# Where the first block tile of each channel mixer prepares the second one's weights

## The chip, the cores and the metric

The kernel runs on one core of a Trainium2 chip. Its time is the device time of one execution in microseconds (us); three executions of the kernel before gave 1180.54, 1180.71 and 1181.04 us, so their median is 1180.71 us. The engines named below are TensorE (PE in the profile, with its weight loads as PEld), VectorE (DVE), ScalarE (ACT), GpSimd (POOL) and SyncE (SP), which issues the loads of weights.

## The reference, cut to what matters

The program is a trunk of two layers over 512 tokens with a model width of 1024, in float32. Each layer has a mixer and then a channel mixer, a gated MLP with a short causal convolution on the gate. The change lies in the channel mixer:

```python
D_FF = ((8 * D_MODEL // 3 + 127) // 128) * 128      # 2816

def causal_dwconv(x, w, b):                         # width 3
    k = w.shape[0]; s = x.shape[1]
    xp = jnp.pad(x, ((0, 0), (k - 1, 0), (0, 0)))
    y = xp[:, 0:s] * w[0]
    for j in range(1, k):
        y = y + xp[:, j:j + s] * w[j]
    return y + b

def conv_ffn(h, w_up, conv_w, conv_b, w_down):
    u, g = jnp.split(h @ w_up, 2, axis=-1)
    g = causal_dwconv(g, conv_w, conv_b)
    return (jax.nn.silu(g) * u) @ w_down

x = x + conv_ffn(rmsnorm(x, norm_ffn_g[l]), ffn_w_up[l], ffn_conv_w[l], ffn_conv_b[l], ffn_w_down[l])
```

## The kernel before

Activations lie with features on the partitions and the 512 tokens along a row. Every float32 operand of a matmul is split into a high part (a cast to fp32r, on ScalarE, line 145) and a low part (the difference, on VectorE, line 146), and one product of two such pairs is three matmuls (lines 201 to 203). The 2816 columns of the hidden width are 22 tiles of 128. Tiles 0 and 1 are computed plainly. Tiles 2 to 21 are **block tiles**: the up and gate weights of a tile, cut into two halves of the 1024 input rows, are four blocks, the activations, cut into two halves of the tokens, are blocks too, and seven block products with sums of blocks (Winograd's form of Strassen's scheme) take the place of eight. In the code a11 and a12 are the halves of the up weights, a22 is a half of the gate weights, and s1 to s4 are the four sums that VectorE forms (line 1048 for each of the four). One block product is 12 matmuls of 256 columns.

`step` (line 966 on) is one block tile. Tile 2 is called the first step here, tile 3 the second, and so on. On TensorE a step is, in this order: a11's product into a PSUM tile r1; a12's into r2; s2's into r1; s1's into r3; s3's into r1; two down products; a22's product into r1; any further down products; s4's product, which adds to r3. The down products belong to `ffn_w_down`: each is a group of 512-column matmuls into a PSUM tile "tr", of which there are two. The first step has four such groups, of six matmuls each, the following steps two. r1 is used four times in a step, so each of its later uses needs ScalarE to have copied the result of the one before out of it (line 983 for the first, line 972 for the others). A "tr" tile is free again when ScalarE has copied it (`add`, line 834), after which GpSimd issues an accumulating DMA of the copy (line 838). r3 is read by VectorE after s1's product (line 1004) and again in the following step (line 1106), and s4's product may not add to it before the first of these reads.

While step j runs, ScalarE and VectorE also **prepare** the weights of tile j + 1 (`Forms`): `sums` forms s1 and s2, `split_second` splits s2, `sum_third` forms s3, `split_up` splits the 1024 columns of a11 and a12, `split_sums` splits s1 and s3 together, `sum_fourth` forms s4, `split_gate` splits a22, and `split_down` splits the tile's down weights. `split_fourth` (s4) stands at the head of the step that uses it. The preparation of the first block tile itself happens during the plain tiles. In the same time the **tail** of tile j − 1 runs (`Tail`): the rest of r3, the scaling by the norm's row, three taps of the convolution (line 770 on ScalarE, two at line 763 on VectorE), silu and the gating. The first step has no tail, since no block tile precedes it; in its place it splits the two hidden rows of the plain tiles.

The channel mixer is written inside a manual schedule: TensorE, ScalarE and VectorE execute their instructions in the order in which the code issues them, each engine in its own queue. So an instruction that waits holds back everything behind it on its engine. SyncE issues the loads as buffers come free.

Of the kernel before, what the change touches and what calls it, by code (L numbers as in the profile page):

```python
# [59 lines left out]
def trunk(  # L60
# [34 lines left out]
    def sb(tag, shape, dtype=F32):  # L95
        count[0] += 1
        return pool.tile(shape, dtype, tag=tag, name=f"{tag}{count[0]}", bufs=bufs[tag])

    def ps(tag):
        count[0] += 1  # L100
        return psum.tile([P, S], F32, tag=tag, name=f"p{tag}{count[0]}", bufs=pbufs[tag])
# [381 lines left out]
    with tc.manual_schedule(engines={mybir.EngineType.PE, mybir.EngineType.Activation, mybir.EngineType.DVE}):  # L483
# [20 lines left out]
        def step(products, os_, k, order):  # L504
            for a, b in order:
                for i, o in enumerate(os_):
                    c = slice(i * P, (i + 1) * P)
                    st, mv = kv[k][a], memT[k][b]
                    first, last = (k, (a, b)) == (0, order[0]), (k, (a, b)) == (KT - 1, order[-1])
                    if products == "keys":  # L510
                        nc.tensor.matmul(o, st[:, c], mv, start=first, stop=last)
                    else:
                        nc.tensor.matmul(o, mv[:, c], st[:, MEM:], start=first, stop=last)
# [12 lines left out]
        first, second = slice(0, MEM), slice(MEM, S)  # L526
# [13 lines left out]
        for q in range(KT // 2):  # L540
            k = 2 * q
            step("keys", ko, k, weights_last if q else ((0, 0), (1, 0), (0, 1)))
            if not q:
                step("values", vo, k, weights_last)
            if q < KT // 2 - 1:
                split(*parts_of[q + 1], memory_rows(q + 1, ("tr", "sc")[q % 2], range(2)))
                for j in (k + 2, k + 3):
                    split(*kv[j], kvraw[j])
            if q:
                step("values", vo, k, weights_last)  # L550
            step("keys", ko, k + 1, weights_last)
            if q == KT // 2 - 1:
                kws1 = [parts(kraw1[0], block=0)]
                keep(0, 0, ko)
                kws1.append(parts(kraw1[1], block=1))
            step("values", vo, k + 1, weights_last)
# [184 lines left out]
    class ChannelMixer:  # L741
# [222 lines left out]
        def step(self, j, w, nxt, tail, plain=None):  # L964
            def then(o, *names):
                for name in names if o is not None else ():
                    getattr(o, name)()

            def sum_products(o, r, w, i):

                self.products(r, w, self.t(i))
                A.copy(o, r[:, :H])  # L972

            new = Tail(self, j)
            late = self.load_late(LATE_ROW[j]) if j in LATE_ROW else None
            then(tail, "last_block", "scaled")
            if tail is not None:
                w.split_fourth()
            then(tail, "scaled_up")
            r1, r2, new.r3 = ps("mm"), ps("mm"), ps("sc")  # L980
            new.up, new.u3, new.pre = sb("t", [P, S]), sb("t", [P, S]), sb("t", [P, S])
            self.products(r1, w.a11, self.b(0, 0), True)
            A.copy(new.up[:, :H], r1[:, :H])
            if tail is None:
                self.keep(plain[0])
                w.split_down()
                V.tensor_tensor(out=plain[1], in0=plain[2], in1=plain[1], op=ALU.mult)
            then(tail, "first_tap", "second_tap", "third_tap")
            self.products(r2, w.a12, self.b(1, 0), True)
            V.tensor_tensor(out=new.up[:, :H], in0=new.up[:, :H], in1=r2[:, :H], op=ALU.add)  # L990
            sum_products(new.up[:, H:], r1, w.s2, 2)
            if tail is None:
                self.keep(plain[1])
                w.split_gate()
                w.split_fourth()
            then(tail, "silu")
            then(nxt, "sums")
            self.products(new.r3, w.s1, self.t(1), True)
            then(tail, "gated")
            then(nxt, "split_second", "sum_third")  # L1000
            sum_products(new.u3[:, :H], r1, w.s3, 3)
            then(tail, "split")
            then(nxt, "split_up")
            V.tensor_tensor(out=new.pre[:, H:], in0=new.u3[:, :H], in1=new.r3[:, :H], op=ALU.add)
            w.down_products(0, 2)
            then(nxt, "split_sums", "sum_fourth")
            w.add_down(0)
            then(nxt, "split_gate")
            w.add_down(1)
            then(nxt, "split_down")  # L1010
            sum_products(new.pre[:, :H], r1, w.a22, 4)
            w.down_products(2, 4)
            self.products(new.r3, w.s4, self.b(1, 1))
            w.add_down(2)
            w.add_down(3)
            if late is not None:
                self.late_row(LATE_ROW[j], late)
            return new, nxt
# [571 lines left out]
    sums = [[] for _ in range(TT)]  # L1590
# [109 lines left out]
```

## Time and profile before

| what | value |
|---|---|
| median of three runs | 1180.71 us |
| the profiled execution | 1180.69 us, its span 1178.7 us |
| TensorE busy | 1162.8 us (99%) |
| VectorE busy | 993.8 us (84%) |
| ScalarE busy | 748.1 us (63%) |
| GpSimd busy | 151.2 us (13%) |
| granted TensorE clock | 0.998 of full speed |
| first step of layer 0 | from 296.3 us of the span, its second step from 315.8 us |
| first step of layer 1 | from 851.3 us of the span |

Times in rows of a timeline are microseconds from the start of the span, followed by the duration of one instruction (or of several that follow each other, counted after an x), and in brackets by the idle time of the engine before it and what ended it. Line numbers are those of the kernel before; the change adds three lines inside `step`, so that line 972 keeps its number, 1004 becomes 1005 and lines from 1048 on become three higher.

### The profile page before, as it was taken

The page shows a single profiled execution, that of the slowest core. Times are in us where ns is not written, and L with a number is a line of the kernel's source. Part 1 is how long each engine was busy: PE and PEld are TensorE (multiplying, and loading weights), DVE is VectorE, ACT ScalarE, POOL GpSimd, SP SyncE. Part 2 cuts the span into 40 slices and gives each one's busy share as a digit, 9 for nine tenths or more (in the row PEclk, how much of TensorE's full clock was granted, in tenths as well). Part 3 has the DMA queues.
Part 4 walks back from the last instruction along what each step waited for, and adds up shares of the span by engine and source line. Part 5 has one row for each costly group of instructions (what it writes and reads, how often), then busy time and mean ns, then how long its engine had stood idle before and what let it go on. Part 6 is the DMA issues. An engine that isn't in the chain of part 4 may idle for free. (4 is left out here: it accounts for less than half of the span.)

```text
span 1178.7 us, 19339 instructions
## 1 busy us (share of the span) xinstructions
PE 1162.8 (99%) x7221; PEld 1036.8 (88%) x7221; DVE 993.8 (84%) x1776; ACT 748.1 (63%) x1347; POOL 151.2 (13%) x254
## 2 busy tenths in 40 slices
PE   9999999999999999999999999999999999999997
PEld 9988888888899999999888888778889999999986
DVE  6777788879899988888798888898989998888865
ACT  6548677657576655555576676776766765555545
POOL 1211101010121222111020000101010111111100
PEclk9999999999999999999999999999999999999999
DMA  8645315244458878776573313235345767777651
GB/s 283 224 110 147 80 55 152 67 152 125 129 155 179 213 174 197 194 172 144 148 218 108 90 55 104 95 95 178 110 133 147 159 148 177 177 179 171 134 162 72
DMA packets 204784, 171.27 MB, mean 145 GB/s; under 512 B 9256, under 2 KB 177934, under 8 KB 204690
## 3 DMA queue, kind: packets, MB, share of 16 engines
q1 hardware_dynamic: 184946, 123.93, 35.7%
q0 software_dynamic: 19168, 45.06, 18.9%
q8 instruction: 56, 0.92, 0.3%
q10 hardware_dynamic: 576, 1.05, 0.2%
q14 instruction: 38, 0.31, 0.1%
HBM read 133.09 MB, written 40.85 MB: 148 GB/s over the span
## 5 line engine op out<-in xcount | busy, mean ns | idle before, releaser
L201 PE MATMUL pmm<-u,wh 128*128 128x256 f32 (+1 forms) x992 | 334.8, 338 | 0.9 <-ACT t L972 0.7
L203 PE MATMUL pmm<-u,wl 128*128 128x256 f32 (+1 forms) x992 | 332.1, 335 | 0.0
L202 PE MATMUL pmm<-u,wh 128*128 128x256 f32 (+1 forms) x992 | 331.8, 334 | 0.0
L146 DVE TENSOR_TENSOR wl<-wr,wh 128x1024 fp32r<-128x1024 f32 (+4 forms) x166 | 186.2, 1122 | 69.6 <-ACT wh L145 69.2
L145 ACT CAST wh<-wr 128x1024 fp32r<-128x1024 f32 (+4 forms) x166 | 160.4, 969 | 71.6 <-PE pmm L202 30.1
L203 PEld LDWEIGHTS pmm<-u,wl 128*128 128x128 f32 x992 | 186.3, 188 | 18.9
L201 PEld LDWEIGHTS pmm<-u,wh 128*128 128x128 f32 x992 | 186.4, 188 | 17.8 <-ACT t L972 1.1
L202 PEld LDWEIGHTS pmm<-u,wh 128*128 128x128 f32 x992 | 186.5, 188 | 16.2 <-DVE u L146 0.5
L201 PE MATMUL ptr<-u,wh 128*128 128x512 f32 x272 | 106.9, 393 | 2.0 <-ACT bias L834 1.0
L202 PE MATMUL ptr<-u,wh 128*128 128x512 f32 x272 | 106.5, 392 | 0.5 <-DVE u L146 0.5
L203 PE MATMUL ptr<-u,wl 128*128 128x512 f32 x272 | 105.8, 389 | 0.0
L145 ACT CAST fh<-pt 128x512 fp32r<-128x512 f32 x120 | 74.8, 625 | 38.5 <-DVE pt L1048 37.2
L201 PE MATMUL pmm<-u,fh 128*128 128x256 f32 x320 | 89.0, 278 | 2.7 <-ACT t L972 2.7
L202 PE MATMUL pmm<-u,fh 128*128 128x256 f32 x320 | 88.6, 277 | 0.0
L972 ACT COPY t<-pmm 128x256 f32<-128x256 f32 x120 | 45.1, 376 | 68.5 <-PE pmm L203 68.4
L203 PE MATMUL pmm<-u,fl 128*128 128x256 f32 x320 | 88.4, 276 | 0.0
L146 DVE TENSOR_TENSOR fl<-pt,fh 128x512 fp32r<-128x512 f32 x120 | 82.4, 688 | 4.6 <-ACT fh L145 1.4
L763 DVE SCALAR_TENSOR_TENSOR t<-t,cols,t 128x511 f32<-128x511 f32 x88 | 65.9, 749 | 10.7 <-ACT t L770 9.2
L201 PEld LDWEIGHTS pmm<-u,fh 128*128 128x128 f32 x320 | 60.1, 188 | 5.6 <-ACT t L972 4.2
L201 PE MATMUL psc<-u,wh 128*128 128x256 f32 (+1 forms) x208 | 63.2, 304 | 0.0
L203 PE MATMUL psc<-u,wl 128*128 128x256 f32 (+1 forms) x208 | 63.0, 303 | 0.0
L202 PE MATMUL psc<-u,wh 128*128 128x256 f32 (+1 forms) x208 | 62.9, 303 | 0.0
(360 smaller groups left out, 2641.3 us busy)
## 6 DMA issues: line engine op xcount, KB each, us to landing
wr<-in_ffn_w_up_dram SPq DMA_DIRECT2D x46, 512.0 KB, 8.2
pt<-in_ffn_w_up_dram SPq DMA_DIRECT2D x40, 512.0 KB, 7.9
wr<-in_ffn_w_down_dram SPq DMA_DIRECT2D x32, 512.0 KB, 5.1
wr<-in_a_w_in_dram SPq DMA_DIRECT2D x20, 512.0 KB, 3.7
xspill<-bias POOLq DMA_DIRECT2D x32, 256.0 KB, 6.9
without_row<-bias POOLq DMA_DIRECT2D x24, 256.0 KB, 4.0
wr<-in_w_kv_dram SPq DMA_DIRECT2D x12, 512.0 KB, 3.8
without_row<-t POOLq DMA_DIRECT2D x24, 256.0 KB, 4.2
```

The costliest lines, as they stand in the source:

```text
L145: high = A.copy(hi, src) if on_act else V.tensor_copy(hi, src)
L146: low = V.tensor_tensor(out=lo, in0=src, in1=f(hi), op=ALU.subtract)
L201: nc.tensor.matmul(o, lh, rh, start=first, stop=False, skip_group_check=more)
L202: nc.tensor.matmul(o, lh, rl, start=False, stop=False, skip_group_check=more)
L203: nc.tensor.matmul(o, ll, rh, start=False, stop=last, skip_group_check=more)
L763: V.scalar_tensor_tensor(acc[:, n:], src[:, : S - n], self.fw[:, c * FT + j : c * FT + j + 1], acc[:, n:], op0=ALU.mult, op1=ALU.add,)
L972: A.copy(o, r[:, :H])
```

## The change

In the first step of each of the two channel mixers, and nowhere else, the preparation of the next tile's weights is issued later. Before, its eight parts were spread over the step: the sums ahead of s1's product, then `split_second` and `sum_third` ahead of s3's product and its copy, and so on. Now seven of them are issued together, behind the copy of s3's product (line 972) and behind the copies of the first two down products (line 834), and the eighth, `split_down`, is issued at the end of the step. `split_up` also comes ahead of `split_second` now. The following steps are as they were. Nothing is added or removed: each engine has the same instructions.

```diff
-            then(nxt, "sums")
+            first, rest = (None, nxt) if tail is None else (nxt, None)
+            then(first, "sums")
             self.products(new.r3, w.s1, self.t(1), True)
             then(tail, "gated")
-            then(nxt, "split_second", "sum_third")
+            then(first, "split_second", "sum_third")
             sum_products(new.u3[:, :H], r1, w.s3, 3)
             then(tail, "split")
-            then(nxt, "split_up")
+            then(first, "split_up")
             V.tensor_tensor(out=new.pre[:, H:], in0=new.u3[:, :H], in1=new.r3[:, :H], op=ALU.add)
             w.down_products(0, 2)
-            then(nxt, "split_sums", "sum_fourth")
+            then(first, "split_sums", "sum_fourth")
             w.add_down(0)
-            then(nxt, "split_gate")
+            then(first, "split_gate")
             w.add_down(1)
-            then(nxt, "split_down")
+            then(rest, "sums", "split_up", "split_second", "sum_third", "split_sums", "sum_fourth", "split_gate")
+            then(first, "split_down")
             sum_products(new.pre[:, :H], r1, w.a22, 4)
             w.down_products(2, 4)
             self.products(new.r3, w.s4, self.b(1, 1))
             w.add_down(2)
             w.add_down(3)
+            then(rest, "split_down")
```

ScalarE's queue in the first step of layer 0, before. The numbers behind a name are buffers: pmm_3215 is r1, the ptr tiles hold the down products, pt_2791 holds the gate weights as loaded and pt_2792 the sums, wr_3015 the up weights of the next tile and wr_3017 its down weights; fh and wh are the high parts.

```order
L145 CAST fh_3277<-pt_2792 128x512
L145 CAST fh_3295<-pt_2792 128x512
L972 COPY t_3219<-pmm_3215 128x256
L145 CAST wh_3313<-wr_3015 128x1024
L145 CAST wh_3332<-pt_2792 128x1024
L834 COPY bias_3337<-ptr_3318 128x512
L145 CAST fh_3340<-pt_2791 128x512
L834 COPY bias_3344<-ptr_3325 128x512
L145 CAST wh_3347<-wr_3017 128x512
L972 COPY t_3220<-pmm_3215 128x256
L834 COPY bias_3390<-ptr_3364 128x512
L834 COPY bias_3393<-ptr_3371 128x512
```

And the same place of ScalarE's queue with the change:

```order
L145 CAST fh_3277<-pt_2792 128x512
L972 COPY t_3219<-pmm_3215 128x256
L834 COPY bias_3321<-ptr_3307 128x512
L834 COPY bias_3324<-ptr_3314 128x512
L145 CAST wh_3329<-wr_3015 128x1024
L145 CAST fh_3333<-pt_2792 128x512
L145 CAST wh_3338<-pt_2792 128x1024
L145 CAST fh_3343<-pt_2791 128x512
L972 COPY t_3220<-pmm_3215 128x256
L834 COPY bias_3386<-ptr_3360 128x512
L834 COPY bias_3389<-ptr_3367 128x512
L145 CAST wh_3392<-wr_3017 128x512
```

The copy of s3's product (t_3219) moved ahead of `split_second` (fh_3295, now fh_3333), and the first two copies of down products ahead of `split_up` and `split_sums`; the cast of the next tile's down weights moved from ahead of the copy of a22's product (t_3220) to the end.

VectorE's queue in the same step, before; lines 1048 are the four sums, line 1004 the first read of r3 (psc_3217), fl and wl the low parts.

```order
L146 TENSOR_TENSOR fl_3278<-pt_2792,fh_3277 128x512
L1048 TENSOR_TENSOR pt_2792<-pt_2791 128x512
L1048 TENSOR_TENSOR pt_2792<-pt_2792,wr_3015 128x512
L146 TENSOR_TENSOR fl_3296<-pt_2792,fh_3295 128x512
L1048 TENSOR_TENSOR pt_2792<-wr_3015,pt_2791 128x512
L146 TENSOR_TENSOR wl_3314<-wr_3015,wh_3313 128x1024
L1004 TENSOR_TENSOR t_3220<-t_3219,psc_3217 128x256
L146 TENSOR_TENSOR wl_3333<-pt_2792,wh_3332 128x1024
L1048 TENSOR_TENSOR pt_2792<-wr_3015,pt_2792 128x512
L146 TENSOR_TENSOR fl_3341<-pt_2791,fh_3340 128x512
L146 TENSOR_TENSOR wl_3348<-wr_3017,wh_3347 128x512
```

And with the change:

```order
L146 TENSOR_TENSOR fl_3278<-pt_2792,fh_3277 128x512
L1005 TENSOR_TENSOR t_3220<-t_3219,psc_3217 128x256
L1051 TENSOR_TENSOR pt_2792<-pt_2791 128x512
L1051 TENSOR_TENSOR pt_2792<-pt_2792,wr_3015 128x512
L146 TENSOR_TENSOR wl_3330<-wr_3015,wh_3329 128x1024
L146 TENSOR_TENSOR fl_3334<-pt_2792,fh_3333 128x512
L1051 TENSOR_TENSOR pt_2792<-wr_3015,pt_2791 128x512
L146 TENSOR_TENSOR wl_3339<-pt_2792,wh_3338 128x1024
L1051 TENSOR_TENSOR pt_2792<-wr_3015,pt_2792 128x512
L146 TENSOR_TENSOR fl_3344<-pt_2791,fh_3343 128x512
L146 TENSOR_TENSOR wl_3393<-wr_3017,wh_3392 128x512
```

The read of r3 moved ahead of all sums, and the low part of the up weights (wl) ahead of the low part of s2 and of the third sum; TensorE, GpSimd and SyncE keep their order.

## The prediction

> **What bounds the kernel now.** I read the page first, then what TensorE waits for, then a table by stretches, then the timelines of the three engines around the first step.
>
> ```profile
> span 1178.7 us, 19339 instructions
> PE 1162.8 (99%) x7221; PEld 1036.8 (88%) x7221; DVE 993.8 (84%) x1776; ACT 748.1 (63%) x1347; POOL 151.2 (13%) x254
> PE pmm L201 <- ACT t L972: 3.4, 4, 1.3
> PE ptr L201 <- ACT bias L834: 1.0, 1, 1.0
> PE ptr L201 <- ACT t L834: 1.0, 1, 1.0
> ```
>
> TensorE is the bound; time is won only where it stands still. The three rows of waits (us in total, times, longest) are the largest it has on other engines in the whole span, and both kinds end on a ScalarE copy that the change moves.
>
> ```profile
> 296.30:314.30 18.00, 15.06 (x97) 12.79 (x96) 15.06 (x22) 10.23 (x17) 1.08 (x2) 1.00 0.26 82
> 326.60:338.90 12.30, 12.30 (x99) 11.81 (x97) 11.69 (x19) 8.44 (x17) 2.24 (x5) 1.00 0.63 177
> ```
>
> Columns: stretch, length, busy time of PE, PEld, DVE, ACT, POOL, granted clock, DMA. The first row holds most of layer 0's first step: TensorE idles 2.94 of 18.00 us. The second is a later step: TensorE never idles, but VectorE is busy for 11.69 of 12.30 us. VectorE is the engine that runs late next.
>
> ```profile
> 306.50 0.69 DVE L1048 TENSOR_TENSOR pt<-pt 128x512 f32<-128x512 f32 x1
> 307.22 0.69 DVE L1048 TENSOR_TENSOR pt<-pt,wr 128x512 f32<-128x512 f32 x1
> 304.56 1.14 ACT L145 CAST fh<-pt 128x512 fp32r<-128x512 f32 x2
> 307.94 0.62 ACT L145 CAST fh<-pt 128x512 fp32r<-128x512 f32 x1 [2.25 <-DVE pt L1048]
> 308.47 0.37 ACT L972 COPY t<-pmm 128x256 f32<-128x256 f32 x1
> 308.73 1.05 ACT L145 CAST wh<-wr 128x1024 fp32r<-128x1024 f32 x1
> 309.98 1.05 ACT L145 CAST wh<-pt 128x1024 fp32r<-128x1024 f32 x1 [0.20 <-DVE pt L1048]
> 310.93 0.58 ACT L834 COPY bias<-ptr 128x512 f32<-128x512 f32 x1
> 311.41 0.62 ACT L145 CAST fh<-pt 128x512 fp32r<-128x512 f32 x1
> 307.16 0.39 PE L203 MATMUL ptr<-u,wl 128*128 128x512 f32 x1
> 308.89 0.38 PE L201 MATMUL pmm<-u,fh 128*128 128x256 f32 x1 [1.34 <-ACT t L972]
> 311.56 0.50 PE L201 MATMUL ptr<-u,wh 128*128 128x512 f32 x1 [1.02 <-ACT bias L834]
> ```
>
> ScalarE waits 2.25 us for VectorE's second sum, and behind that cast stands the copy of r1 (308.47) for which TensorE waits 1.34 us with a22's product. Two long casts later comes the copy of a down product (310.93), for which TensorE waits 1.02 us with the third group. Layer 1 has the same waits (the counts above).
>
> **What the change removes.** The copy of r1 now follows the two casts of 304.56 and ends near 306.0, before TensorE is there. The first two copies of down products follow at once. So TensorE goes on from its last row of the second group (307.16) without either wait. How much earlier would the second step begin if nothing else were late? Its rows are these; the rows of the other engines are for the next part:
>
> ```profile
> 315.82 0.28 PE L201 MATMUL pmm<-u,wh 128*128 128x256 f32 x1
> 326.74 0.28 PE L201 MATMUL psc<-u,fh 128*128 128x256 f32 x1
> 328.10 0.28 PE L201 MATMUL pmm<-u,wh 128*128 128x256 f32 x1
> 311.29 1.22 DVE L146 TENSOR_TENSOR wl<-pt,wh 128x1024 fp32r<-128x1024 f32 x1
> 312.42 0.68 DVE L1048 TENSOR_TENSOR pt<-wr,pt 128x512 f32<-128x512 f32 x1
> 316.02 0.42 DVE L1106 TENSOR_TENSOR t<-t,psc 128x256 f32<-128x256 f32 x1 [0.20 <-PE psc L203]
> 316.36 0.68 DVE L1109 TENSOR_TENSOR t<-t,rb 128x512 f32<-128x512 f32 x1
> 316.96 0.68 DVE L146 TENSOR_TENSOR fl<-pt,fh 128x512 fp32r<-128x512 f32 x1
> 317.65 0.82 ACT L770 ACTIVATE t<-t,cols 128x512 f32<-128x512 f32 x1
> 318.50 1.54 DVE L763 SCALAR_TENSOR_TENSOR t<-t,cols,t 128x511 f32<-128x511 f32 x2 [0.85 <-ACT t L770]
> 319.96 0.41 DVE L990 TENSOR_TENSOR t<-t,pmm 128x256 f32<-128x256 f32 x1
> 320.29 0.68 DVE L1048 TENSOR_TENSOR pt<-pt 128x512 f32<-128x512 f32 x1
> 321.01 0.69 DVE L1048 TENSOR_TENSOR pt<-pt,wr 128x512 f32<-128x512 f32 x1
> 322.38 0.69 DVE L146 TENSOR_TENSOR fl<-pt,fh 128x512 fp32r<-128x512 f32 x1
> 324.70 1.23 DVE L146 TENSOR_TENSOR wl<-wr,wh 128x1024 fp32r<-128x1024 f32 x1 [0.26 <-ACT wh L145]
> 325.84 0.41 DVE L1004 TENSOR_TENSOR t<-t,psc 128x256 f32<-128x256 f32 x1
> ```
>
> The second step runs from 315.82 to 328.10: 12.28 us. Its s4 product, 12 matmuls of 256 columns, takes 1.36 (326.74 to 328.10); seven such products are 9.52, which leaves 2.76 for its two down groups, 0.23 for each of 12 matmuls. From 307.16 the new first step then goes: 0.23 to a22's product at 307.39; 1.36; two more down groups, 2.76; s4's product, 1.36; and the second step begins at 312.87 instead of 315.82. That is 2.95 us, more than the 2.36 of the two idle times, since a wait also slows the matmul behind it (0.38 against 0.28 at 308.89).
>
> **What is late next.** VectorE has the same work to do in less time, and its preparation now starts later, behind ScalarE's copies. I time the new order with the old durations. An instruction lets the next start after 0.60 (512 columns: 316.36 to 316.96), 1.13 to 1.14 (1024: 311.29 to 312.42, 324.70 to 325.84) or 0.33 (256: 319.96 to 320.29) on VectorE; a wait across engines adds 0.03 to 0.05 (316.36 + 0.68 = 317.04 would release the tap; 317.65 + 0.82 = 318.47, and VectorE starts at 318.50).
>
> - The second down group ends at 307.16 + 0.39 = 307.55. ScalarE copies it at 307.58 and casts the up weights 0.48 later (as 310.93 to 311.41): 308.07 to 309.11.
> - VectorE, which has read r3 and made two sums by 308.3, waits for that cast: low part of the up weights at 309.15, low part of s2 at 310.29, third sum 310.89 to 311.58.
> - ScalarE's cast of s1 and s3 waits for that third sum, 311.62 to 312.67, and VectorE's low part for the cast: 312.70. Then without a gap: fourth sum 313.84, gate 314.44, down weights 315.05, rest of r3 315.65, scaling 315.98 to 316.67.
> - Tap on ScalarE 316.71 to 317.53; two taps on VectorE from 317.56, 1.46 to the next (318.50 to 319.96): line 990 at 319.02, first sum 319.35, second (0.72 later, as at 320.29) 320.07 to 320.76; cast on ScalarE, low part of s2 at 321.46; third sum, low part of the hidden row and low part of the up weights at 322.06, 322.66 and 323.27; read of r3 at 324.41, done at 324.82.
>
> Before, that read (line 1004) was at 325.84, done at 326.25, and TensorE came to s4's product at 326.74: 0.44 to spare after the release. Now TensorE would be there at 312.87 + 10.92 = 323.79 and has to wait until 324.87, 1.08 us in all. (A part falls earlier in the step. On ScalarE, behind the cast of 311.62, stand the gate's cast, the copy of a22's product, two copies of down products and two casts: 0.95 + 0.53 + 0.26 + 2 × 0.48 + 2 × 0.53 by the starts above. So the first copy of r1 in the second step comes at 315.4, done at 315.75, while TensorE is due with s2's product at 312.87 + 2.72 = 315.59. Some 0.2 us are waited there and are then missing from the second wait.) s4's product starts 326.74 − 324.87 = 1.87 us earlier than before; two waits slow two matmuls by 0.10 each, of which one counts behind it, with a slightly slower pace. I take **1.7 us per mixer**.
>
> From the third step on VectorE can gain on TensorE. One round of its chain, with the links above, is 0.34 + 1.57 (scaling, tap) + 1.46 + 0.33 + 0.72 + 1.38 (second sum, cast) + 3 × 0.60 + 1.14 + 0.33 + 1.14 + 3 × 0.60 = 12.01 us against TensorE's 12.28. It is 0.27 us ahead again in the next step, so no further wait follows.
>
> Everything else that moves is covered. The copies of the third and fourth down group (near 313.4 and 313.9) free tiles that TensorE wants again only after three products of the second step. The copy of a22's product starts at 311.62 + 0.95 + 0.53 = 313.10, is done at 313.5, and r1's buffer is next written at 314.2. On SyncE nothing is reordered, but loads start when VectorE frees buffers:
>
> ```profile
> 306.01 0.37 SPq L857 DMA_DIRECT2D pt<-in_ffn_w_up_dram x1
> DMA to landing us min/median/max: 3.7/8.0/11.6
> DMA to landing us min/median/max: 3.1/4.8/9.4
> ```
>
> Tile 4's gate weights are still issued at 306.01 and wanted at 319.35: 13.3 us, against at most 11.6 for loads of this tensor (second row). Its down weights wait for the fourth sum, done at 314.5 instead of 313.1, and are cast at 325.5: 11 us, against at most 9.4 (third row).
>
> **The sum.** 2.95 − 1.08 − 0.15 is 1.7 per mixer, 3.4 for two, since both mixers have the same order and waits. The profiled execution took 1180.69 us, within 0.02 of the median 1180.71, so the forecast is **1177.3 us**. A difference below 0.2%, 2.4 us, can't be told from none here. Bounds of what the trace doesn't show: VectorE's chain could cost nothing (2.95 per mixer), or half a microsecond more than I count (1.2 per mixer); I stay with the chain as timed, since its links are all rows.
>
> **Rivals.**
> - *Nothing is late.* VectorE closes up (it had 0.85 us idle at 318.50) and TensorE never waits: 2 × 2.95 = 5.9 us, 1174.8. Against it: that 0.85 is in my chain already, and the chain has 1.08 too much. Chance 0.07.
> - *The gain is mostly given back.* If the chain is 0.55 us later per mixer, or the third to seventh step wait a little too, under 2.4 us remain: about 1179. For it: a VectorE loop of 12.01 against 12.28 is a thin margin. Against: in the old steps it holds. Chance 0.14.
> - *GpSimd's issue holds VectorE.* The third and fourth accumulating DMAs are now issued near 314.0 and 314.5, inside the tight chain. If each held VectorE for its duration, 1.08 per mixer would go, leaving 2 × 0.6: 1179.5. Row against it:
>
> ```profile
> 316.15 1.07 POOL L838 DMA_DIRECT2D without_row<-bias  x2 [2.80 <-ACT bias L834]
> ```
>
> While GpSimd issued these two, VectorE's instructions at 316.36 and 316.96 took 0.68 each, no longer than elsewhere. Chance 0.02. [...]
> - *VectorE becomes the bound* (slower). Place: s4's product in the second to seventh step of each mixer, where the reading of r3 releases it. Price: what VectorE's loop has over 12.28 us, in each of five steps behind the second. It decides from a loop of 12.28, and the kernel is slower than before once five steps give back 1.7, from 12.62; at 12.9 it gives back 3.1 per mixer, and the time is 1180.7 + 2.8 = 1183.5. For it: 11.69 busy of 12.30. Against: the loop by rows is 12.01. Chance 0.03.
>
> That the change doesn't do what it says is ruled out by the order of the queues: the copies do stand ahead.
>
> **How the numbers follow.** Forecast 0.74 (its own range 1176.5 to 1178.2), rivals 0.07, 0.14, 0.02 and 0.03. Faster by over 0.2% are the forecast and the first rival: 0.80, a little kept back for what I haven't seen; within 0.2% 0.16; slower 0.04. The range takes in the forecast and most of the second rival, and goes halfway to the first: 1175.6 to 1178.8.
>
> **What would show it.** Right: no wait of TensorE on lines 972 or 834 in the first steps; the second step begins near 312.9 and 867.8; a wait of 0.2 us at its s2 product and of about 0.8 us at its s4 product, the latter on VectorE's line 1005; the third step begins near 326.4 instead of 328.10; every later step 1.7, then 3.4 us earlier. Wrong: no wait at s4's product (1174.8), waits at s4 in further steps, or a load that VectorE's sums or ScalarE's cast of down weights wait for.

## The result, and the profile after

The changed kernel takes 1178.27 us (median of 17 runs, 1177.67 to 1179.56), the kernel before 1180.54 us (17 runs beside them, 1179.98 to 1181.83). The ratio is 0.9981, with a 95% interval of 0.9974 to 0.9989: 2.3 us faster, where 3.4 were forecast. The direction and the mechanism came out as predicted; a third of the gain is missing. 1178.27 lies in the predicted range, 1175.6 to 1178.8, but 0.07 us outside the narrower one of the forecast itself (1176.5 to 1178.2), and a gain of 0.19% is among the outcomes "within 0.2%", which were given a chance of 0.16.

The first lines of the page after, and from the table of TensorE's waits the rows on the block tiles of the two channel mixers (us in total, times, longest):

```profile
span 1176.1 us, 19341 instructions
PE 1162.6 (99%) x7221; PEld 1036.5 (88%) x7221; DVE 992.7 (84%) x1776; ACT 747.7 (64%) x1347; POOL 151.2 (13%) x254
PE psc L201 <- DVE t L1005: 1.3, 2, 0.9
PE pmm L201 <- ACT t L972: 0.9, 2, 0.5
PE pmm L201 <- ACT t L983: 0.2, 1, 0.2
```

Line 834 is gone from the waits, and line 972 has only its two other waits, which the first steps had before too (its four waits were 3.4 us together). New is line 1005, the reading of r3, with one wait in each mixer, and line 983, the copy of r1 for which s2's product waits. (Behind the changed place the changed kernel's line numbers are 1 to 3 higher.)

How far TensorE is ahead is read from the starts of its products. These are its rows in the changed kernel, first mixer: first step, second step, s4's product in it, third step, third step's first down group.

```profile
295.77 0.28 PE L201 MATMUL pmm<-u,wh 128*128 128x256 f32 x1
312.30 0.28 PE L201 MATMUL pmm<-u,wh 128*128 128x256 f32 x1
324.39 0.39 PE L201 MATMUL psc<-u,fh 128*128 128x256 f32 x1 [0.44 <-DVE t L1005]
325.91 0.28 PE L201 MATMUL pmm<-u,wh 128*128 128x256 f32 x1
333.05 0.39 PE L201 MATMUL ptr<-u,wh 128*128 128x512 f32 x1
```

In the kernel before, the first step starts at 296.32 and that down group at 334.90:

```profile
296.32 0.28 PE L201 MATMUL pmm<-u,wh 128*128 128x256 f32 x1
334.90 0.40 PE L201 MATMUL ptr<-u,wh 128*128 128x512 f32 x1
```

Counted from each execution's own first step (the two differ by 0.55 us already there, which the change can't have made), TensorE is ahead by:

| at | predicted | first mixer | second mixer |
|---|---|---|---|
| second step | 2.95 | 2.97 | 2.95 |
| s4's product | 1.87 | 1.80 | 1.44 |
| third step | 1.70 | 1.64 | 1.26 |
| third step's down group | 1.70 | 1.30 | 0.93 |

(The row "second step" in the first mixer: 315.82 - 296.32 before, 312.30 - 295.77 now, 19.50 - 16.53; the others likewise.) Behind the last row nothing more is lost within a mixer, and some 0.2 us are lost between the mixers: 1.30 + 0.93 - 0.2 = 2.0. So the gain went in three places: 0.34 us in the third step of each mixer, where TensorE doesn't wait at all; 0.4 more ahead of s4's product in the second mixer; and 0.2 in a place that the change doesn't touch.

### The profile page after: what moved, and what is told of

It reads as the page before. It is cut to its first block, busy times and chain, and to the rows that moved or that the text cites. A ratio compares the mean times of both kernels' runs of the same rounds, so it can differ in the third digit from the quotient of the medians.

```text
span 1176.1 us, 19341 instructions
## 1 busy us (share of the span) xinstructions
PE 1162.6 (99%) x7221; PEld 1036.5 (88%) x7221; DVE 992.7 (84%) x1776; ACT 747.7 (64%) x1347; POOL 151.2 (13%) x254
## 4 chain that ended last, share of the span: by engine, by line
PE 83%; DVE 10%; ACT 4%; issue 2%; DMA 1%; SPq 0%; POOL 0%; DVEq 0%; ACTq 0%; POOLq 0%
PE pmm L201 16%; PE pmm L202 16%; PE pmm L203 16%; PE ptr L202 6%; PE ptr L203 5%; PE ptr L201 5%; PE psc L201 4%; PE psc L202 4%; PE psc L203 4%; PE psc L620 2%; DVE wl L146 2%; PE ptr L1525 1%; ACT wh L145 1%; DVE t L807 1%; DVE u L146 1%
```

## The experiments

**Does the second step's wait cost what it seems to?** Two kernels are built to take the new waits away without undoing the change. In the first, VectorE reads r3 before it makes the low part of the up weights, in every step:

```diff
             then(tail, "split")
-            then(first, "split_up")
             V.tensor_tensor(out=new.pre[:, H:], in0=new.u3[:, :H], in1=new.r3[:, :H], op=ALU.add)
+            then(first, "split_up")
```

> The change, and in every step VectorE's reading of r3 (line 1005) now stands ahead of the low part of the up weights (1.22 us, one to the next 1.14). In the second step of each mixer the reading then ends 1.1 us earlier, ahead of TensorE, so that the wait at s4's product is gone; the wait at s2's product (0.39) stays. Theory A (the removal is worth 2.95 us per mixer, and what is missing in the changed kernel is its two waits and a slower run of the 256-column matmuls behind a wait, 0.119 us from one to the next instead of 0.113, until a down group of 512 columns ends it: 72 matmuls, 0.43 us behind s4's): gain 2.95 - 0.35 - 0.10 = 2.5 per mixer, 1180.5 - 5.0 = 1175.5; behind s4's product the pace is 0.113. Theory B (the slower pace isn't caused by the wait but by the denser work of the other engines there): the wait goes, the pace stays, 2.07 per mixer, 1176.4. Theory C (the removal itself was worth less than 2.95): the wait's own length is all there is to win, 1178.3 - 0.44 - 0.9 = 1177.0.

Measured: 1176.33 us (1175.59 to 1176.95; before beside it 1180.43), ratio 0.9964 (0.9952 to 0.9977). The wait at s4's product is gone from the table, and by TensorE's starts both mixers gain 2.4 us. Behind s4's product the pace is 0.113 us. The time alone would fit theory B (1176.4), but its slower pace isn't there, and 2.4 per mixer is near A's 2.5, not B's 2.07. A's 1175.5 is 0.8 too low; 0.28 of it is the loss between the mixers, told below, and the rest isn't explained (the profiled execution also waited 1.0 us at 26.5 us, on line 453, far ahead of the changed place).

In the second kernel the seven moved steps have another order:

```diff
-            then(rest, "sums", "split_up", "split_second", "sum_third", "split_sums", "sum_fourth", "split_gate")
+            then(rest, "sums", "split_second", "sum_third", "split_up", "split_sums", "sum_fourth", "split_gate")
```

> The change with another order of the seven moved steps: s2's high and low part and the third sum stand ahead of the up weights' parts. ScalarE's cast of s1 and s3 then finds the third sum done (it waited 2.03 us), VectorE doesn't wait 1.17 us for that cast, and scaling and tap of the second step come about 1 us earlier. By the rows' durations neither s2's nor s4's product waits. Theory A: no wait, so no slower pace behind one: the whole 2.95 us per mixer, 1180.5 - 5.9 = 1174.6. Theory B (the slower pace comes from the denser work of the other engines): 2.95 - 0.5 per mixer, 1175.6. Theory C (the removal was worth less than 2.95, or VectorE is late in some later step): 1177 or more.

Measured: 1175.18 us (1174.87 to 1175.73), ratio 0.9956 (0.9943 to 0.9968). The first mixer keeps the whole 2.92 from its second step on. The second mixer has 2.95 up to s4's product and 2.32 at the next down group. Its rows there, the last matmul ahead of s4's product and the first ones of it:

```profile
875.21 0.28 PE L203 MATMUL pmm<-u,fl 128*128 128x256 f32 x1
875.45 0.39 PE L201 MATMUL psc<-u,fh 128*128 128x256 f32 x1
875.67 0.28 PE L202 MATMUL psc<-u,fh 128*128 128x256 f32 x1
```

From 875.21 to 875.45 is 0.24 instead of 0.113: TensorE waited 0.12 us for the reading of r3 (874.98 + 0.41 on VectorE), too little for the profile to call it a wait. The next matmul starts 0.22 later, and the 70 behind it follow at 0.119: 0.12 + 0.11 + 70 x 0.0056 = 0.62. So a wait of 0.12 us cost 0.6. By the rows theory A holds for both mixers, with this one wait that the durations hadn't shown; the time, 1175.18, lies between A's 1174.6 and B's 1175.6.

With both orders together there should be no wait left in the second step:

> The two orders of the runs before together: third sum ahead of the up weights' parts among the seven moved steps, and VectorE's reading of r3 ahead of the low part of the up weights in every step. Theory A (a wait of TensorE in the second step is all that the change loses, with the pace that some waits leave behind): with the third sum first the second mixer still waited 0.12 us at s4's product and then ran 70 matmuls at 0.119 us; with the reading 1.1 us earlier that goes too, and both mixers gain what the first did, 2.93: 1180.45 - 5.9 = 1174.6, and no slow pace in the second steps. Rival (the low part of the up weights, now 0.33 later, is late for the third step's first product, or the second mixer loses its 0.6 for another reason): 1175.2 or more.

Measured: 1174.83 us (1174.16 to 1176.38; before 1180.42), ratio 0.9952 (0.9938 to 0.9965). TensorE's rows in the first mixer, first step, second step, s4's product, third step and its down group:

```profile
296.40 0.28 PE L201 MATMUL pmm<-u,wh 128*128 128x256 f32 x1
312.94 0.28 PE L201 MATMUL pmm<-u,wh 128*128 128x256 f32 x1
323.86 0.28 PE L201 MATMUL psc<-u,fh 128*128 128x256 f32 x1
325.22 0.28 PE L201 MATMUL pmm<-u,wh 128*128 128x256 f32 x1
332.02 0.40 PE L201 MATMUL ptr<-u,wh 128*128 128x512 f32 x1
```

The five products from 325.22 to 332.02 take 6.80 us, as before the change (328.10 to 334.90); in the changed kernel they take 7.14 (325.91 to 333.05). That is the 0.34 us: 60 matmuls at 0.119 instead of 0.113, with no wait among them and the granted clock at 1.00. The gain is 2.96 in the first mixer and 2.87 in the second, at all four points of the table. So the removal was worth what was predicted, and the rest is the second step's waits and the pace behind them. This version beats both kernels.

**Is the slower pace made by every wait?** In the kernel before, the reading of r3 is put later in the steps of tiles 4 and 6:

```diff
-            V.tensor_tensor(out=new.pre[:, H:], in0=new.u3[:, :H], in1=new.r3[:, :H], op=ALU.add)
+            if j not in (4, 6):
+                V.tensor_tensor(out=new.pre[:, H:], in0=new.u3[:, :H], in1=new.r3[:, :H], op=ALU.add)
...
-            then(nxt, "split_sums", "sum_fourth")
+            then(nxt, "split_sums")
+            if j == 4:
+                V.tensor_tensor(out=new.pre[:, H:], in0=new.u3[:, :H], in1=new.r3[:, :H], op=ALU.add)
+            then(nxt, "sum_fourth")
             w.add_down(0)
             then(nxt, "split_gate")
+            if j == 6:
+                V.tensor_tensor(out=new.pre[:, H:], in0=new.u3[:, :H], in1=new.r3[:, :H], op=ALU.add)
```

> The kernel before, with VectorE's reading of r3 put later in the third and fifth step of the loop of each mixer (tiles 4 and 6): in the one behind the low part of s1 and s3, in the other behind the gate's low part too. By the rows' durations TensorE then waits 0.72 us at s4's product of the one and 1.93 of the other. Nothing else is changed. Theory A (a wait slows the one matmul behind it by 0.10, and all 256-column matmuls from 0.113 to 0.119 until the next down group, 72 of them, 0.43 us): 0.72 + 1.93 + 2 x 0.53 = 3.7 per mixer, 1180.5 + 7.4 = 1187.9. Theory B (a wait costs its length and 0.10, the slower pace has another cause): 2.85 per mixer, 1186.2. If the pace follows only waits under a microsecond or so, 3.3 per mixer, 1187.1, and the rows behind the second wait show 0.113.

Measured: 1186.57 us (1186.25 to 1186.68), ratio 1.0051 (1.0037 to 1.0064). The new waits in the table:

```profile
PE psc L201 <- DVE t L1014: 3.5, 2, 1.7
PE psc L201 <- DVE t L1009: 1.1, 2, 0.5
```

From start to start, less the usual 0.113, they are 0.71 us and 1.91. Behind three of the four the pace is 0.113, behind one (0.71 us, second mixer) 0.119 up to the down group. 6.1 us lie near theory B's 5.7, and A falls as I put it: a wait can leave the slower pace behind, but need not, and its length doesn't decide it.

**What ends the slower pace?** In the change, the third step's first two down groups are issued ahead of s1's product instead of behind s3's:

```diff
+            if j == PLAIN + 2:
+                w.down_products(0, 2)
             self.products(new.r3, w.s1, self.t(1), True)
...
-            w.down_products(0, 2)
+            if j != PLAIN + 2:
+                w.down_products(0, 2)
```

> The change, and in the third step (tile 4) of each mixer the first two down groups, 24 matmuls of 512 columns, stand ahead of s1's product on TensorE, 24 products of 256 columns earlier. The slow pace behind s4's product of the second step lasted 70 matmuls in both mixers of the changed kernel, up to these groups. Theory (a down group ends it): 0.119 us for 46 matmuls, up to the groups, and 0.113 for the 24 of s1 and s3 behind them, 0.13 us less lost per mixer where it occurs. Rival (it ends by time or by count): s1 and s3 still at 0.119 behind the groups.

Measured: 1182.04 us (one run; before 1180.42). This run missed its aim: behind s4's product of the second step the pace was 0.113 in both mixers this time, after waits of 0.6 us, like the one that was followed by 0.119 in the first mixer of the changed kernel. The moved groups made new waits in the third step, and s4's product there waited as well:

```profile
PE psc L201 <- DVE t L1007: 3.6, 4, 1.4
PE pmm L201 <- ACT t L972: 1.9, 4, 0.5
```

What it adds is to the count. Over all kernels, 26 waits (0.12 to 2.5 us) stand ahead of a product of 256 columns with at least 34 such matmuls behind it and no fall of the clock. After 17 of them the pace was 0.119, after 9 it was 0.113, and in all 17 it was 0.113 again behind the next down group. What chooses between the two is open, and that the down group itself ends it isn't shown by an experiment. Outside this count there are cases against it: in the run with both orders, the run with another buffer and the last run below, a22's product in the second mixer's first step ran at 0.118 to 0.119 behind down groups with a wait of 0.5 us inside. In the other kernels it ran at 0.114 wherever it had no wait of its own, behind the same groups. That is why the second mixer gains 2.87 and not 2.95 with both orders.

**What is a copy worth on its own?** The kernel before with one half of the change, first the copy of r1 alone:

```diff
-            then(nxt, "split_second", "sum_third")
-            sum_products(new.u3[:, :H], r1, w.s3, 3)
+            if tail is None:
+                sum_products(new.u3[:, :H], r1, w.s3, 3)
+                then(nxt, "split_second", "sum_third")
+            else:
+                then(nxt, "split_second", "sum_third")
+                sum_products(new.u3[:, :H], r1, w.s3, 3)
```

> The kernel before, with one part of the change: in the first step ScalarE's cast of s2 and VectorE's third sum stand behind the copy of r1 (line 972 of the kernel before); the two copies of down products (line 834) still stand behind the casts of the up weights and of s1 and s3. Theory A (both waits come from one chain: ScalarE's casts end when they end, and TensorE meets that end at line 834 if not at 972): the wait on line 972 is gone, the one on line 834 grows to about 2.7 us, and the time is that of before, 1180.5. Rival (each wait is worth its own length): 1.34 + 0.1 per mixer, 1177.6.

Measured: 1184.62 us (1183.87 to 1186.17), ratio 1.0038 (1.0025 to 1.0050), slower by 4.2. Both theories are wrong on the time. As theory A said, the wait moves to line 834 with 2.7 us. But the rows behind it, and the table by stretches for 3.7 us from that wait's end in each mixer (columns as in the prediction), show something else:

```profile
311.27 0.50 PE L201 MATMUL ptr<-u,wh 128*128 128x512 f32 x1 [2.68 <-ACT bias L834]
311.61 0.47 PE L202 MATMUL ptr<-u,wh 128*128 128x512 f32 x1
311.87 0.63 PE L203 MATMUL ptr<-u,wl 128*128 128x512 f32 x1
312.30 0.63 PE L201 MATMUL ptr<-u,wh 128*128 128x512 f32 x1
312.73 0.63 PE L202 MATMUL ptr<-u,wh 128*128 128x512 f32 x1
311.20:314.90 3.70, 3.63 (x10) 2.86 (x11) 2.20 (x3) 1.02 (x3) 1.08 (x2) 0.58 0.51 146
867.90:871.60 3.70, 3.50 (x8) 2.79 (x9) 2.33 (x3) 1.15 (x3) 1.08 (x2) 0.54 0.50 142
```

A matmul of 512 columns takes 0.43 us from start to start instead of 0.23, and the granted clock is 0.58 and 0.54: behind the single long wait TensorE's clock fell. The second step begins 1.6 us later than before, and at a pace of 0.119 up to its down groups it loses 0.3 more, 2.0 per mixer. The kernel before, with the same idle time cut in two by a product (1.34 and 1.02), kept a granted clock of 1.00.

Then the copies of down products alone:

```diff
-            then(nxt, "split_up")
+            first, rest = (None, nxt) if tail is None else (nxt, None)
+            then(first, "split_up")
             V.tensor_tensor(out=new.pre[:, H:], in0=new.u3[:, :H], in1=new.r3[:, :H], op=ALU.add)
             w.down_products(0, 2)
-            then(nxt, "split_sums", "sum_fourth")
+            then(first, "split_sums", "sum_fourth")
             w.add_down(0)
-            then(nxt, "split_gate")
+            then(first, "split_gate")
             w.add_down(1)
+            then(rest, "split_up", "split_sums", "sum_fourth", "split_gate")
```

> The kernel before, with the other part of the change: in the first step the two copies of down products (line 834) stand ahead of the casts of the up weights and of s1 and s3, but the sums, the cast of s2 and the third sum stay ahead of the copy of r1. Theory A (durations of the rows): the wait on r1's copy stays (1.5 us with its slowed matmul), the one on the down copy goes, with it 1.27 us per mixer; the sums are made early, so VectorE isn't late in the second step: 1180.45 - 2.5 = 1177.9, as much as the whole change gave, since that loses in the second step what it wins on r1's copy. Rival (the casts, now behind the copies, make VectorE late there as in the change): a wait at s4's product again, 1179 or more.

Measured: 1177.97 us (1177.42 to 1178.52), ratio 0.9979 (0.9970 to 0.9988). Line 972 keeps its four waits, line 834 and line 1005 have none:

```profile
PE pmm L201 <- ACT t L972: 3.4, 4, 1.3
```

TensorE is 1.34 and 1.28 us ahead from the second step on in the two mixers and loses nothing later. Theory A holds: this half alone gives as much as the whole change.

**From how long a wait does the clock fall?** In the kernel before, longer waits at the same two products as above: the reading of r3 behind the gate's low part and done twice (tile 4), and behind the down weights' low part (tile 6); it is taken out of its old place in both, as there.

```diff
             then(nxt, "split_gate")
+            if j == 4:
+                V.tensor_tensor(out=new.pre[:, H:], in0=new.u3[:, :H], in1=new.r3[:, :H], op=ALU.add)
+            if j == 4:
+                V.tensor_tensor(out=new.pre[:, H:], in0=new.u3[:, :H], in1=new.r3[:, :H], op=ALU.add)
             w.add_down(1)
             then(nxt, "split_down")
+            if j == 6:
+                V.tensor_tensor(out=new.pre[:, H:], in0=new.u3[:, :H], in1=new.r3[:, :H], op=ALU.add)
```

> The kernel before, with waits of TensorE made longer than in the run with 0.71 and 1.91 us: in the step of tile 4 VectorE's reading of r3 stands behind the gate's low part and is done twice with the same result (wait 2.37 us by the rows), in the step of tile 6 it stands behind the down weights' low part (2.53 us). Theory A (the clock that TensorE is granted falls to about 0.58 for 4 us behind a wait that is long enough, which 1.91 us weren't and 2.84 us were): if both are long enough each costs its length and some 1.7 us, 1180.45 + 2 x (4.9 + 0.2 + 3.4) = 1197.5; if neither, 1190.7; if the longer alone, 1194.1. Rival (the fall came from the product behind that wait, of 512 columns, or from that place in the program): granted clock 1.00 behind both, 1190.7.

Measured: 1195.86 us (one run), near 1190.7 and three falls at 1.7, 1195.8. Stretches of 3.7 us behind the four waits (2.37 us, 2.51 us, and the same in the second mixer):

```profile
340.80:344.50 3.70, 3.49 (x17) 3.49 (x18) 1.28 (x4) 0.00 (x0) 0.00 (x0) 0.54 0.99 172
369.50:373.20 3.70, 3.48 (x30) 3.48 (x31) 1.79 (x4) 0.45 (x2) 0.00 (x0) 1.00 1.00 179
902.30:906.00 3.70, 3.44 (x21) 3.44 (x22) 2.43 (x5) 0.00 (x0) 0.00 (x0) 0.74 1.07 287
931.20:934.90 3.70, 3.46 (x16) 3.46 (x17) 0.68 (x3) 0.00 (x0) 0.00 (x0) 0.54 1.01 223
```

The clock fell behind both waits of 2.37 us (in the third row it falls later within the stretch, hence 0.74) and behind one of the two of 2.51; behind 1.91 us it fell in neither mixer. So the length of a wait alone doesn't decide it. The rival falls: these products have 256 columns and stand in another place.

The records of the granted clock in the traces show more. Each of the five falls (three here, two in the run with the copy of r1 alone) lasts 3.41 us at 0.50. Those of one execution begin whole multiples of 3.413 us apart: here at 340.87, 904.07 and 931.37, 165 and 8 times. On this grid the stretch that ends where the second fall begins, and the fall:

```profile
900.65:904.07 3.42, 1.51 (x12) 1.51 (x13) 2.42 (x5) 1.21 (x3) 0.54 (x1) 1.00 0.81 244
904.07:907.48 3.41, 3.41 (x18) 3.41 (x17) 1.62 (x3) 0.58 (x2) 0.00 (x0) 0.50 1.07 290
```

TensorE was idle for 1.91 us of that stretch, and for 2.06, 2.29, 2.67 and 2.68 ahead of the other falls. The grid cuts the wait of 2.51 us that had no fall in two (0.79 and 1.55 us idle by the profile); one of the waits of 1.91 us lies whole in a stretch, but is only 1.75 us idle by the profile. Over the traces of all kernels here, from 20 us on, a fall followed every grid stretch with 1.91 us of idle time or more and none with 1.87 or less. In the kernel before, the record of full clock lasts 1167.36 us, 342 times 3.4133; on the grid from its start the most that one stretch holds of the two waits is 1.76 us of idle time (307.56 to 310.97, TensorE busy for 1.65 of 3.41), and the granted clock stayed at 1.00 in it and behind it.

**Why did the second mixer gain less?** ScalarE's tap of the second step, and on VectorE the scaling it waits for and the reading of r3, in the changed kernel: the first mixer, then the second.

```profile
315.46 0.69 DVE L1112 TENSOR_TENSOR t<-t,rb 128x512 f32<-128x512 f32 x1
316.24 0.82 ACT L770 ACTIVATE t<-t,cols 128x512 f32<-128x512 f32 x1 [1.02 <-DVE t L1112]
323.92 0.41 DVE L1005 TENSOR_TENSOR t<-t,psc 128x256 f32<-128x256 f32 x1
869.34 0.69 DVE L1112 TENSOR_TENSOR t<-t,rb 128x512 f32<-128x512 f32 x1
870.40 0.82 ACT L770 ACTIVATE t<-t,cols 128x512 f32<-128x512 f32 x1 [1.30 <-DVE t L1112]
878.09 0.41 DVE L1005 TENSOR_TENSOR t<-t,psc 128x256 f32<-128x256 f32 x1
```

The tap starts 0.09 us behind the end of the scaling in the first mixer (316.15), and 0.37 in the second (870.03). The 0.28 stay in the chain: from scaling to reading it is 8.46 us and 8.75. The two kernels with one other order each have the same two gaps, 0.09 and 0.37. First suspect was the tap's output buffer:

```diff
-            t = sb(("bias", "t")[self.l], [P, S])
+            t = sb("t" if self.l and q > 3 else "bias", [P, S])
```

> The change, and in the second mixer the copies of down products of the first four steps go to buffers of the tag that the first mixer uses for them, not to those of the hidden rows. In the second mixer the tap (line 770) of the second step starts 0.32 us after its engine's wait for the scaling has ended, in the first mixer 0.05, in each of three kernels. Theory (the buffer: the tap's output buffer is one that a GpSimd transfer of a down product still reads): the gap becomes 0.05, s4's product waits 0.3 us less in the second mixer. Rival (something else of that instruction, such as its place in the program): the gap stays 0.32.

Measured: 1179.18 us (one run), and the tap of the second mixer again starts 0.37 behind its scaling (870.34 + 0.69):

```profile
871.40 0.82 ACT L770 ACTIVATE t<-t,cols 128x512 f32<-128x512 f32 x1 [1.29 <-DVE t L1112]
```

It isn't the buffer. Second suspect was the place of the instruction in ScalarE's program:

```diff
                 ou = run(self.plain_chain(1, True, w2))
+                if self.l:
+                    A.copy(sb("s0", [P, 16])[:, :1], self.fb[:, :1])
```

> The change, and in the second mixer, ahead of its first step, one more copy of one column by ScalarE to a tile that nothing reads, so that every later instruction of ScalarE stands one place further on. The buffer was not the cause of the 0.32 us between the end of the wait and the tap in the second mixer. Theory (its place in ScalarE's program): the gap in front of the tap of the second step becomes about 0.05, since another instruction, one that waits anyway, now stands at that place; VectorE's chain is 0.27 us earlier and s4's product waits less, about 0.75 instead of 1.07 with its slowed matmul. Rival (something of this instruction's operands or waits): 0.32 again.

Measured: 1179.18 us (one run). The tap starts 0.09 behind its scaling (870.28 + 0.69 = 870.97), and s4's product comes 0.63 us behind its turn, where it was 1.07 (its lead is 1.70 instead of 1.44; the rest is that TensorE came to it later, at the slower pace this time):

```profile
871.06 0.82 ACT L770 ACTIVATE t<-t,cols 128x512 f32<-128x512 f32 x1 [1.02 <-DVE t L1114]
```

So it is the place. The same shows between the mixers, at ScalarE's line 1514 of the changed kernel (line 1511 before; the four rows are ScalarE before and after, then what waits for it on VectorE before and after):

```profile
787.84 0.40 ACT L1511 ACTIVATE t<-t,s 128x128 f32<-128x128 f32 x1 [1.11 <-DVE s L1507]
786.19 0.40 ACT L1514 ACTIVATE t<-t,s 128x128 f32<-128x128 f32 x1 [1.38 <-DVE s L1510]
788.38 0.16 DVE L1512 RECIPROCAL s<-s 128x1 f32<-128x1 f32 x1 [0.42 <-ACT t L1511]
786.72 0.16 DVE L1515 RECIPROCAL s<-s 128x1 f32<-128x1 f32 x1 [0.69 <-ACT t L1514]
```

It starts 0.27 us later behind its releaser than before, and VectorE waits 0.27 longer. By count it stands 128 of ScalarE's recorded instructions ahead of the second mixer's tap. The last kernel joins both orders with the one-column copy, now in the first mixer, ahead of both places (the line of the diff above with `self.l == 0`):

> The kernel with both orders (third sum first, reading of r3 ahead of the up weights' low part), and the one-column copy by ScalarE to a tile that nothing reads, now in the first mixer. In the changed kernel and in every kernel built on it with the same number of ScalarE's instructions, an instruction of line 1514 between the mixers started 0.32 us after the end of its wait, 0.05 in the kernel before and in the run of the down copies alone, and all three engines were 0.26 us later behind it; it stands 128 of ScalarE's recorded instructions ahead of the tap of the second mixer that was late too. Theory (place in ScalarE's program): with one more instruction ahead of it that instruction starts 0.05 behind its wait, TensorE keeps its 0.26, and the tap of the second mixer starts 0.05 behind its wait: 1174.8 - 0.25 = 1174.55, hardly to be told from 1174.8 by the times, but by the rows. Rival (the two are late for another reason): 0.32 at both again.

Measured: 1174.47 us (1173.81 to 1174.90; before 1180.40), ratio 0.9949 (0.9936 to 0.9963). The row between the mixers:

```profile
784.49 0.40 ACT L1516 ACTIVATE t<-t,s 128x128 f32<-128x128 f32 x1 [1.10 <-DVE s L1512]
```

It waits 1.10 as before the change; TensorE, which lost 0.17 to 0.28 between the mixers in the kernels with other orders, loses nothing there, and the tap starts 0.05 behind the end of its wait (0.09 behind the scaling). The theory holds in both places. It is the fastest of all kernels here, though the 0.4 us to the kernel without the copy can't be told from none by the times.

## Why the prediction was nearly right

- **The removal, 2.95 per mixer: right.** Measured 2.97 and 2.95, and 2.96 and 2.87 to the end of the mixer where no wait follows. But it is not the sum of what two copies are worth: the down copies alone give 1.3, the copy of r1 alone -2.0.
- **What is late next: right in place and size in the first mixer.** VectorE's reading of r3 was predicted to end at 324.82 by the old clock; it ended at 324.33 in an execution that was 0.55 earlier, 324.88. s4's product was 1.80 us ahead where 1.87 were forecast. The part at s2's product fell as forecast too (some 0.2; 0.26 us from start to start). In the second mixer the same chain was 0.36 us worse, of which 0.28 is the tap's place in ScalarE's program. That step rested on "both mixers have the same order and waits", and this failed: same order, another place.
- **"Two waits slow two matmuls by 0.10 each, of which one counts behind it, with a slightly slower pace" - the step that failed.** It was the 0.15 in the sum. The slowed matmuls and s4's own 12 cost 0.16 and 0.18 up to the third step, as counted. But the slower pace went on through the third step's five products, 0.34 us in each mixer: the term measured 0.50. So long a slow stretch doesn't occur in the profile of before, but the pace itself does, in the first step: its s1 product there, first and last matmul, takes 0.118 us from one to the next.

```profile
300.53 0.28 PE L201 MATMUL psc<-u,wh 128*128 128x256 f32 x1
301.83 0.28 PE L203 MATMUL psc<-u,wl 128*128 128x256 f32 x1
```

- **No further wait from the third step on: right.** Behind the third step's down group TensorE's lead is constant within each mixer.
- **The loads, the other copies: right.** No transfer stands among TensorE's waits in the block tiles of the two channel mixers.
- **GpSimd's issue doesn't hold VectorE: right.** GpSimd issues the third and fourth transfer while VectorE runs at its usual 0.69 and 0.68:

```profile
313.72 1.07 POOL L838 DMA_DIRECT2D without_row<-bias  x2 [5.28 <-ACT bias L834]
313.92 0.69 DVE L146 TENSOR_TENSOR fl<-pt,fh 128x512 fp32r<-128x512 f32 x1
314.53 0.68 DVE L146 TENSOR_TENSOR wl<-wr,wh 128x512 fp32r<-128x512 f32 x1
```

- **The sum.** With what was measured it is (1.70 - 0.40) + (1.70 - 0.77) - 0.2 = 2.0 in the profiled executions, and 2.3 by the medians, against 3.4. The second rival (gain mostly given back, 1179) was near in size, but not for its reason: the VectorE chain was as late as counted in the first mixer and 0.36 later in the second, where the rival wanted 0.55, and no later step waits. That the range held in spite of the missing third owes something to having been stretched to take in this rival. Nothing was left out on the side of the gain: with both other orders it is 5.6 us, and 5.9 with the one-column copy.
- **One reading of the profile was off.** TensorE's three waits weren't the largest it had on other engines: line 490 waits 1.1 us for VectorE, before the change and after it. It lies elsewhere, and the sum doesn't use it.

## What to carry to other kernels

Moving a blocked copy forward moves the lateness to whatever stood behind it (here TensorE then waited 0.44 and 0.91 us at s4's product for VectorE's reading of r3), so order the moved work by who is waited for next: the same seven steps with the third sum first, and the reading of r3 ahead of the up weights' low part in every step, gave more than twice the gain. Count with a short wait of TensorE what can follow it, up to half a microsecond here (a wait of 0.12 us cost 0.62), and don't merge two short waits into one long one: here 2.7 us of idle time in one piece cost 2.0 us more per mixer than 1.3 and 1.0 in two.

## What was not expected of the hardware

- Behind a wait, even of 0.12 us, TensorE's matmuls of 256 columns ran at 0.119 us instead of 0.113, at a granted clock of 1.00, up to the next group of 512 columns, after 17 waits of 26. What decides it, and what ends it, is open.
- The granted clock fell to 0.50 for 3.41 us behind single waits of 2.4 us (two of two), 2.5 (one of two) and 2.8 (two of two), and not behind 1.9 (two). In these traces it went with the idle time within one stretch of a grid of 3.413 us: behind 1.91 us or more it fell, behind 1.87 or less it didn't.
- A ScalarE instruction that had just been released started 0.32 us after its wait instead of 0.05, at two places 128 instructions apart in its program; one instruction more ahead of them, and both started at 0.05. Whether it recurs every 128 instructions, and what lies behind it, no run here shows. In the changed kernel the queue q14, listed as "instruction", made 38 transfers of 8192 bytes each, one for about 127 of the 4809 recorded instructions of ScalarE, VectorE, GpSimd and SyncE; whether the late starts have to do with them, no run tests.
